# Scores of gated linear attention in three products of 128 columns per chunk

## The chip, the cores and the metric

The kernel runs on one core of a Trainium2 chip. The core has TensorE (PE, with its weight loads shown as PEld), VectorE (DVE), ScalarE (ACT), GpSimd (POOL) and SyncE (SP), which here issues all DMAs. The metric is the device time of one execution in microseconds; lower is better.

## What is computed

One layer of a hybrid backbone: a normalised input is projected once into eleven parts, from which a bidirectional gated linear attention (GLA, four heads of 128 key channels) and a differential attention are computed, gated, merged and projected out. The change concerns the scores inside a chunk of GLA, for one direction:

```python
cum = jnp.cumsum(log_a, axis=3)                       # chunks of 64 positions
ref = cum[:, :, :, GLA_CHUNK // 2 - 1:GLA_CHUNK // 2]
scores = jnp.einsum('bhnid,bhnjd->bhnij', q * jnp.exp(cum - ref), k * jnp.exp(ref - cum))
o_intra = jnp.einsum('bhnij,bhnjv->bhniv', jnp.where(tri, scores, 0.0), v)
o_inter = ...                                         # from the state carried between chunks
o = o_intra + o_inter                                 # forward; backward the same on reversed streams; the two are added
```

There are 1024 latent tokens and 256 context tokens, all in fp32.

## The kernel before

The kernel works with chunks of 128 positions, cut into two sub-chunks `s` of 64. A head has ten chunks, two of context and eight of latent tokens. The latent ones are worked on in pairs, `g` = 1 to 4, and `e` is the direction (0 forward, 1 backward). For a pair the scores of both directions are masked, added and stored to DRAM (`d_sc`) as one array of 128 x 128 per chunk.

A small planner writes the order of the instructions. Every task is a Python generator that says what it waits for; the planner keeps an estimated clock for each engine, and the order in which tasks are woken is the order of the instructions on TensorE, ACT, DVE and POOL. On the chip each engine then works its list off in that order, and semaphores hold it where an operand is late. Between the tasks of GLA, TensorE works on the stream of projections (tiles `mm`, `ma`, `tp`), which has the lowest priority and fills the gaps. Buffers are counted by tag: `acq` waits for a free one, `rel` gives it back. `TAGS` gives each tag its pool and number of buffers.

GLA's first part (`gla_a`, with the tiles of pool `sbG`) has these tasks for each head. `scans` forms the cumulated decays `cf` (forward) and `eb` (backward). `kstates` and `queries` form the operands of the carried state. `factors` subtracts a sub-chunk's reference from the decays (`gd` for a sub-chunk's own reference, `gx` for the other one's), `rest` takes Exp on ACT and multiplies with queries (`gqr`) and keys (`gkk`) on DVE or POOL, whichever the planner expects to be done first (`either`). `scores` then multiplies on TensorE into one PSUM bank `gs`, copies it to `gsc` on ACT, masks it on POOL (`affine_select`), adds the directions and stores. Before, a score product is 128 x 64: all of a chunk's keys, in the form that one sub-chunk of queries needs (its own block, the block beside the diagonal, zeros elsewhere), times that sub-chunk's queries. Eight such products serve a pair (two directions, two chunks, two sub-chunks). `gsc`, `gd` and `gx` have one buffer.

When the last scores are stored (`ev_ga`), `sums7` starts: it adds and subtracts blocks of the input activations for a stage of seven products per weight matrix, where TensorE uses `gs`, `go`, `gt` and `ma` for four tiles at a time. Its operand `s2` overwrites the second half of the activations (`h`); if the projections before it still need that half, `s2` goes to DRAM and is fetched back later. The first of the seven products is evacuated by ACT, the second is added to `us` and `rope` by DVE, the third is the one with `s2`.

Of the kernel before, what the change touches and what calls it, by code (L numbers as in the profile page):

```python
# [12 lines left out]
AF = mybir.ActivationFunctionType  # L13
ALU = mybir.AluOpType
# [5 lines left out]
P = 128  # L20
# [6 lines left out]
TAU = 1.0 / 16  # L27
# [218 lines left out]
class Hybrid:  # L246
# [10 lines left out]
        gk=("sbG", 2), gq=("sbG", 1), glab=("sbG", 2), glaf=("sbG", 2), gsc=("sbG", 1), gtl=("sbG", 4), gm=("sbG", 1),  # L257
        **{f"{t}{e}": ("sbG", n) for t, n in dict(ge=2, gkt=2, gqe=2, gqr=2, gkk=2, gd=1, gx=1).items() for e in range(2)},
# [1256 lines left out]
    def gla_a(self):  # L1515

        d = self.d
        H = [dict() for _ in range(4)]
        ev_s = {(h, e): Event() for h in range(4) for e in range(2)}
        ev_r = {(h, g, e): Event() for h in range(4) for g in range(1, 5) for e in range(2)}  # L1520
# [111 lines left out]
        def factors():  # L1632

            for h in range(4):
# [5 lines left out]
                for g in range(1, 5):  # L1640
                    for e in range(2):
                        sl = slice(2 * g, 2 * g + 2)
                        q4 = st["gq"][:, 2 * g - 2:2 * g].rearrange("p c (s t) -> p c s t", t=64)
                        k4 = st["gk"][:, sl].rearrange("p c (s t) -> p c s t", t=64)
                        cc = st["eb" if e else "cf"][:, sl].rearrange("p c (s t) -> p c s t", t=64)
                        ref = cc[:, :, :, 32:33] if e else cc[:, :, :, 31:32]
                        for tg in ("gd", "gx", "gqr", "gkk"):
                            yield from self.acq(f"{tg}{e}")
                        dd = self.t(f"gd{e}", [P, 2, 2, 64])
                        yield On(0, "DVE")  # L1650
                        for s in range(2):
                            self.dve.tensor_tensor(dd[:, :, s], cc[:, :, s], ref[:, :, s].to_broadcast([P, 2, 64]),
                                                   ALU.subtract)
                        xd = self.t(f"gx{e}", [P, 2, 64])
                        r_ = ref[:, :, 1 - e].to_broadcast([P, 2, 64])
                        x = (cc[:, :, 1], r_) if e else (r_, cc[:, :, 0])
                        self.dve.tensor_tensor(xd, *x, ALU.subtract)
                        qq = self.t(f"gqr{e}", [P, 2, 2, 64])
                        kk = self.t(f"gkk{e}", [P, 2, 4, 64])
                        self.pool.memset(kk[:, :, 2 if e else 1], 0.0)  # L1660
                        d.spawn(rest(h, g, e, dd, xd, qq, kk, q4, k4), d.on("ACT", dd), prio=2)

        def rest(h, g, e, dd, xd, qq, kk, q4, k4):
            sg = -1.0 if e else 1.0
            self.act.activation(qq, dd, AF.Exp, scale=sg * TAU)
            self.act.activation(dd, dd, AF.Exp, scale=-sg * TAU)
            self.act.activation(xd, xd, AF.Exp, scale=TAU)
            yield d.when(qq, H[h]["gq"])
            self.either(qq, q4, qq, ALU.mult)
            yield d.when(dd, H[h]["gk"])  # L1670
            self.rel(f"gd{e}", self.either(kk[:, :, 0:4:3], k4, dd, ALU.mult))
            yield d.when(xd)
            self.rel(f"gx{e}", self.either(kk[:, :, 1 if e else 2], k4[:, :, e], xd, ALU.mult))
            ev_r[h, g, e].qk = qq, kk
            d.set(ev_r[h, g, e], d.when(qq, kk))

        def scores():

            for h in range(4):
                for g in range(1, 5):  # L1680
                    for e in range(2):
                        yield ev_r[h, g, e]
# [997 lines left out]
```

## Time and profile before

| | us |
|---|---|
| median of three runs (1685.82 to 1686.82) | 1686.13 |
| the profiled execution | 1685.7 |
| its span | 1684.0 |
| TensorE busy | 1631.7 |
| VectorE busy | 1208.2 |
| ScalarE busy | 819.1 |
| GpSimd busy | 647.8 |

The profile is of one execution. Times in its timeline run from the start of the span; a row groups consecutive instructions of one kind, and its length reaches to the modelled end of the last one, so the pace is read from start to start. On TensorE an fp32 product of the scores is two records. What stands in brackets is idle time ahead of the row and the work whose end ended it.

### The profile page before, as it was taken

How to read it: one execution, taken by the hardware profiler on the slowest of the kernel's cores; microseconds unless marked ns; L12 is line 12 of the kernel's file. 1: busy time of each engine (PE TensorE's matmuls, PEld its weight loads, DVE VectorE, ACT ScalarE, POOL GpSimd, SP SyncE). 2: the span in 40 equal slices, each digit the busy share in tenths (PEclk: the TensorE clock that was granted, in tenths of full speed). 3: DMA queues.
4: the chain of work that ended last, by engine and by line, in shares of the span. 5: the costliest groups of instructions: out<-in, count | busy, mean ns of one | idle time of the engine just before them, and what ended most of it. 6: DMA issues, size and time to landing. Idle time of an engine off the chain costs nothing.

```text
span 1684.0 us, 24646 instructions
## 1 busy us (share of the span) xinstructions
PE 1631.7 (97%) x8381; PEld 1354.1 (80%) x8381; DVE 1208.2 (72%) x1940; ACT 819.1 (49%) x1633; POOL 647.8 (38%) x659
## 2 busy tenths in 40 slices
PE   8999999999999999999999989999999999999999
PEld 3688887888788878888888778888888888878887
DVE  4766867866855465857776658897888888847694
ACT  4786545454342434343332346665666565642231
POOL 1600542552310013435444625565655656630000
PEclk9999999999999999999999999999999999999999
DMA  8547554653754474459899663443784534257422
GB/s 312 204 154 238 172 165 164 190 160 125 232 170 138 143 237 140 143 174 279 270 301 314 184 196 107 111 128 85 222 262 114 157 105 125 66 180 251 152 99 75
DMA packets 266431, 296.58 MB, mean 176 GB/s; under 512 B 23577, under 2 KB 186305, under 8 KB 266305
## 3 DMA queue, kind: packets, MB, share of 16 engines
q1 hardware_dynamic: 266304, 295.01, 56.0%
q8 instruction: 66, 1.08, 0.3%
q14 instruction: 61, 0.49, 0.1%
HBM read 195.84 MB, written 99.09 MB: 175 GB/s over the span
## 4 chain that ended last, share of the span: by engine, by line
PE 71%; DVE 11%; POOL 5%; issue 4%; ACT 3%; DMA 2%; SPq 0%; ACTq 0%; POOLq 0%; DVEq 0%
PE mm L353 16%; PE mc L353 10%; PE ma L353 9%; PE s L353 6%; PE mb L353 6%; PE b L353 5%; PE gs L353 5%; DVE sm L211 4%; PE go L353 3%; PE b L379 3%; PE gt L353 3%; DVE e L211 2%; PE tp L353 2%; ACT e L211 2%; POOL p L211 2%
## 5 line engine op out<-in xcount | busy, mean ns | idle before, releaser
L211 DVE TENSOR_REDUCE sm<-s 128x1 f32<-128x1024 f32 (+1 forms) x192 | 197.3, 1037 | 33.1 <-PE s L353 32.5
L353 PE MATMUL mm<-w,h 128*128 128x512 f32 x864 | 216.9, 400 | 3.0 <-DVE w L211 2.3
L211 ACT ACTIVATE e<-s,sm 128x1280 f32<-128x1280 f32 x128 | 170.2, 1331 | 85.5 <-DVE sm L211 75.6
L353 PEld LDWEIGHTS mm<-w,h 128*128 128x128 f32 x864 | 160.7, 189 | 38.0 <-DVE w L211 2.6
L211 POOL TENSOR_TENSOR at<-ac,at 128x512 fp32r<-128x512 f32 x128 | 186.0, 1453 | 10.7
L353 PE MATMUL s<-kk,aq 128*128 128x512 f32 (+1 forms) x768 | 173.9, 360 | 6.9 <-ACT e L211 6.9
L353 PE MATMUL mb<-h,wt 128*128 128x512 f32 x624 | 170.5, 404 | 4.8 <-DVE ft L211 3.2
L211 POOL TENSOR_SCALAR at<-ac 128x512 fp32r<-128x512 f32 x128 | 97.5, 761 | 186.9 <-ACT ac L211 181.5
L353 PE MATMUL mm<-h,w 128*128 128x512 f32 x624 | 154.6, 398 | 0.0
L353 PEld LDWEIGHTS s<-kk,aq 128*128 128x128 f32 x768 | 121.0, 188 | 26.3 <-ACT e L211 10.7
L353 PEld LDWEIGHTS mm<-h,w 128*128 128x128 f32 x624 | 116.7, 191 | 24.1 <-DVE h L211 0.4
L353 PE MATMUL b<-at,vv 128*128 128x256 f32 x960 | 129.6, 283 | 1.9 <-DVE at L211 1.4
L353 PEld LDWEIGHTS mb<-h,wt 128*128 128x128 f32 x624 | 109.7, 188 | 25.2 <-DVE ft L211 4.3
L353 PEld LDWEIGHTS b<-at,vv 128*128 128x128 f32 x960 | 120.9, 188 | 7.4 <-POOL at L211 2.6
L211 POOL TENSOR_TENSOR sm<-sm,nhalf 128x8 f32<-128x8 f32 (+3 forms) x78 | 105.4, 1351 | 30.7 <-DVE sm L211 25.3
L353 PE MATMUL mc<-h,wt 128*128 128x512 f32 x480 | 113.1, 396 | 1.6 <-DVE wt L211 1.6
L211 DVE SCALAR_TENSOR_TENSOR e<-e,sm,e 128x1280 f32<-128x1280 f32 x64 | 112.4, 1756 | 1.2
L353 PEld LDWEIGHTS mc<-h,wt 128*128 128x128 f32 x480 | 90.9, 190 | 22.2 <-DVE wt L211 2.5
L211 ACT ACTIVATE ac<-b 128x512 f32<-128x512 f32 x121 | 71.9, 598 | 57.3 <-PE b L379 54.9
L353 PE MATMUL ma<-w,h 128*128 128x512 f32 x384 | 96.6, 396 | 0.4 <-DVE gp L211 0.4
L379 PE MATMUL b<-ident,e 128*128 128x128 f32 x604 | 87.6, 273 | 6.9 <-DVE at L211 3.1
L379 PEld LDWEIGHTS b<-ident,e 128*128 128x128 f32 x604 | 72.5, 141 | 23.8 <-ACT ac L211 3.9
(385 smaller groups left out, 3177.6 us busy)
## 6 DMA issues: line engine op xcount, KB each, us to landing
raw<-in_w_in SPq DMA_DIRECT2D x37, 512.0 KB, 4.7
rb<-in_w_in SPq DMA_DIRECT2D x64, 256.0 KB, 3.0
aq<-d_qT SPq DMA_DIRECT2D x128, 128.0 KB, 4.0
d_kT<-pl SPq DMA_DIRECT2D x40, 256.0 KB, 2.4
d_dv<-pl SPq DMA_DIRECT2D x40, 256.0 KB, 2.1
kk<-d_kT SPq DMA_DIRECT2D x32, 320.0 KB, 4.8
gv<-d_v SPq DMA_DIRECT2D x40, 256.0 KB, 4.5
vv<-d_dv SPq DMA_DIRECT2D x16, 640.0 KB, 6.6
```

What stands on the lines that cost most here:

```text
L211: self.ins = f(out, *args, **kw).ins
L353: self.ins = self.nc.tensor.matmul(out, lhsT, rhs, start=start, stop=stop, skip_group_check=more).ins
L379: self.nc.tensor.transpose(out, src, self.ident[:n, :n])
```

## The change

The factors of both directions now lie in joint tiles: `qq` [128, chunk, direction, sub-chunk, 64], `kk` the same, and `xx` [128, chunk, direction, 64] for the block beside the diagonal. Per chunk there are three products of 128 columns: for each direction all keys times all queries, each with its own sub-chunk's reference (only the two diagonal blocks of it are used), and one that holds the blocks beside the diagonal of both directions: 64 columns of keys of each direction, times the queries `q[:, 64:192]`, the forward second sub-chunk and the backward first one. A half pair (`j`) takes the bank `gs`, ACT copies the two full products and then, over them, the two 64 x 64 blocks of the third. So the bank is taken twice per pair, and emptied in six copies. The zeroing of parts of `gkk` falls away, and `gd` with it: the differences are formed in `kk`. `gsc`, `gqr`, `gkk` and `gx` have two buffers each.

```diff
@@ -254,8 +254,9 @@
 
         s7=("sbS", 24), ra=("sbS", 4), rb=("sbS", 3), us=("sbS", 2), rc=(None, 4), **{f"u{x}": (None, 1) for x in range(12)},
 
-        gk=("sbG", 2), gq=("sbG", 1), glab=("sbG", 2), glaf=("sbG", 2), gsc=("sbG", 1), gtl=("sbG", 4), gm=("sbG", 1),
-        **{f"{t}{e}": ("sbG", n) for t, n in dict(ge=2, gkt=2, gqe=2, gqr=2, gkk=2, gd=1, gx=1).items() for e in range(2)},
+        gk=("sbG", 2), gq=("sbG", 1), glab=("sbG", 2), glaf=("sbG", 2), gsc=("sbG", 2), gtl=("sbG", 4), gm=("sbG", 1),
+        gqr=("sbG", 2), gkk=("sbG", 2), gx=("sbG", 2),
+        **{f"{t}{e}": ("sbG", 2) for t in ("ge", "gkt", "gqe") for e in range(2)},
 
         bkt0=("sbA2", 2), bkt1=("sbA2", 2), gv0=("sbA2", 3), gv1=("sbA2", 3), bqe=("sbA2", 2), bsc=("sbA2", 3), bg=("sbA2", 3),
         gsb0=("sbA2", 8), gsb1=("sbA2", 8), gsf=("sbA2", 4), gs1=("sbA2", 1), gp=("sbA2", 4), gpl=("sbA2", 4),
@@ -1517,7 +1518,7 @@
         d = self.d
         H = [dict() for _ in range(4)]
         ev_s = {(h, e): Event() for h in range(4) for e in range(2)}
-        ev_r = {(h, g, e): Event() for h in range(4) for g in range(1, 5) for e in range(2)}
+        ev_r = {(h, g): Event() for h in range(4) for g in range(1, 5)}
         heads = [Event() for _ in range(4)]
         for h in range(4):
             for e in range(2):
@@ -1638,72 +1639,80 @@
                 while "gq" not in st:
                     yield At(d.now + 2.0)
                 for g in range(1, 5):
+                    for tg in ("gkk", "gx", "gqr"):
+                        yield from self.acq(tg)
+                    kk = self.t("gkk", [P, 2, 2, 2, 64])
+                    xx = self.t("gx", [P, 2, 2, 64])
+                    qq = self.t("gqr", [P, 2, 2, 2, 64])
                     for e in range(2):
-                        sl = slice(2 * g, 2 * g + 2)
-                        q4 = st["gq"][:, 2 * g - 2:2 * g].rearrange("p c (s t) -> p c s t", t=64)
-                        k4 = st["gk"][:, sl].rearrange("p c (s t) -> p c s t", t=64)
-                        cc = st["eb" if e else "cf"][:, sl].rearrange("p c (s t) -> p c s t", t=64)
+                        cc = st["eb" if e else "cf"][:, 2 * g:2 * g + 2].rearrange("p c (s t) -> p c s t", t=64)
                         ref = cc[:, :, :, 32:33] if e else cc[:, :, :, 31:32]
-                        for tg in ("gd", "gx", "gqr", "gkk"):
-                            yield from self.acq(f"{tg}{e}")
-                        dd = self.t(f"gd{e}", [P, 2, 2, 64])
+                        own = [cc, ref.to_broadcast([P, 2, 2, 64])]
+                        far = [ref[:, :, 1 - e].to_broadcast([P, 2, 64]), cc[:, :, e]]
                         yield On(0, "DVE")
-                        for s in range(2):
-                            self.dve.tensor_tensor(dd[:, :, s], cc[:, :, s], ref[:, :, s].to_broadcast([P, 2, 64]),
-                                                   ALU.subtract)
-                        xd = self.t(f"gx{e}", [P, 2, 64])
-                        r_ = ref[:, :, 1 - e].to_broadcast([P, 2, 64])
-                        x = (cc[:, :, 1], r_) if e else (r_, cc[:, :, 0])
-                        self.dve.tensor_tensor(xd, *x, ALU.subtract)
-                        qq = self.t(f"gqr{e}", [P, 2, 2, 64])
-                        kk = self.t(f"gkk{e}", [P, 2, 4, 64])
-                        self.pool.memset(kk[:, :, 2 if e else 1], 0.0)
-                        d.spawn(rest(h, g, e, dd, xd, qq, kk, q4, k4), d.on("ACT", dd), prio=2)
-
-        def rest(h, g, e, dd, xd, qq, kk, q4, k4):
-            sg = -1.0 if e else 1.0
-            self.act.activation(qq, dd, AF.Exp, scale=sg * TAU)
-            self.act.activation(dd, dd, AF.Exp, scale=-sg * TAU)
-            self.act.activation(xd, xd, AF.Exp, scale=TAU)
+                        self.dve.tensor_tensor(kk[:, :, e], *own[::-1 if e else 1], ALU.subtract)
+                        yield On(0, "DVE")
+                        self.dve.tensor_tensor(xx[:, :, e], *far[::-1 if e else 1], ALU.subtract)
+                    d.spawn(rest(h, g, kk, xx, qq), d.on("ACT", xx), prio=2)
+
+        def rest(h, g, kk, xx, qq):
+            k = H[h]["gk"][:, 2 * g:2 * g + 2]
+            both = lambda x: x.unsqueeze(2).to_broadcast([P, 2, 2, P])
+            flat = lambda x: x.rearrange("p c e s t -> p c e (s t)")
+            self.act.activation(qq, kk, AF.Exp, scale=TAU)
+            self.act.activation(kk, kk, AF.Exp, scale=-TAU)
+            self.act.activation(xx, xx, AF.Exp, scale=TAU)
             yield d.when(qq, H[h]["gq"])
-            self.either(qq, q4, qq, ALU.mult)
-            yield d.when(dd, H[h]["gk"])
-            self.rel(f"gd{e}", self.either(kk[:, :, 0:4:3], k4, dd, ALU.mult))
-            yield d.when(xd)
-            self.rel(f"gx{e}", self.either(kk[:, :, 1 if e else 2], k4[:, :, e], xd, ALU.mult))
-            ev_r[h, g, e].qk = qq, kk
-            d.set(ev_r[h, g, e], d.when(qq, kk))
+            self.either(flat(qq), both(H[h]["gq"][:, 2 * g - 2:2 * g]), flat(qq), ALU.mult)
+            yield d.when(kk, H[h]["gk"])
+            self.either(flat(kk), both(k), flat(kk), ALU.mult)
+            yield d.when(xx)
+            xf = xx.rearrange("p c e t -> p c (e t)")
+            self.either(xf, k, xf, ALU.mult)
+            ev_r[h, g].qk = qq, kk, xx
+            d.set(ev_r[h, g], d.when(qq, kk, xx))
 
         def scores():
+
+            def evac(j, psc, sc, after):
+                act = self.act.activation
+                act(sc[:, :, j], psc[:, 0:2], AF.Copy)
+                act(sc[0:64, 0, j, 64:128], psc[0:64, 2, 0:64], AF.Copy)
+                self.rel("gs", act(sc[64:128, 1, j, 0:64], psc[64:128, 2, 64:128], AF.Copy))
+                if j:
+                    d.spawn(after(sc), d.on("POOL", sc), prio=2)
+                return
+                yield
 
             for h in range(4):
                 for g in range(1, 5):
-                    for e in range(2):
-                        yield ev_r[h, g, e]
-                    yield from self.acq("gs")
-                    psc = self.t("gs", [P, 2, 2, 2, 64])
-                    for e in range(2):
-                        qq, kk = ev_r[h, g, e].qk
-                        for j in range(2):
-                            for s in range(2):
-                                en = self.mm(psc[:, e, j, s], kk[:, j, 2 * s:2 * s + 2].rearrange("p a b -> p (a b)"),
-                                             qq[:, j, s], True, True)
-                        self.rel(f"gqr{e}", en)
-                        self.rel(f"gkk{e}", en)
-                    yield On(en, "ACT")
+
+                    def sums(sc, h=h, g=g):
+                        for e in range(2):
+                            sg = -1 if e else 1
+                            self.pool.affine_select(sc[:, e], sc[:, e], pattern=[[0, 2], [sg, P]], compare_op=ALU.is_ge,
+                                                    fill=0.0, base=0, channel_multiplier=-sg)
+                        yield d.when(sc)
+                        self.either(sc[:, 0], sc[:, 0], sc[:, 1], ALU.add)
+                        self.store([(self.d_sc[h][:, 2 * g - 2:2 * g], sc[:, 0])], ("gsc", 1), ev=self.ev_st["sc", 0, h, g])
+                        finished(h)
+
+                    yield ev_r[h, g]
+                    qq, kk, xx = ev_r[h, g].qk
                     yield from self.acq("gsc")
                     sc = self.t("gsc", [P, 2, 2, P])
-                    en = self.act.activation(sc, psc.rearrange("p e j s t -> p e j (s t)"), AF.Copy)
-                    self.rel("gs", en)
-                    yield On(en, "POOL")
-                    for e in range(2):
-                        sg = -1 if e else 1
-                        self.pool.affine_select(sc[:, e], sc[:, e], pattern=[[0, 2], [sg, P]], compare_op=ALU.is_ge,
-                                                fill=0.0, base=0, channel_multiplier=-sg)
-                    yield d.when(sc)
-                    self.either(sc[:, 0], sc[:, 0], sc[:, 1], ALU.add)
-                    self.store([(self.d_sc[h][:, 2 * g - 2:2 * g], sc[:, 0])], ("gsc", 1), ev=self.ev_st["sc", 0, h, g])
-                    finished(h)
+                    for j in range(2):
+                        yield from self.acq("gs")
+                        psc = self.t("gs", [P, 3, P])
+                        q = qq[:, j].rearrange("p e s t -> p (e s t)")
+                        for e in range(2):
+                            self.mm(psc[:, e], kk[:, j, e].rearrange("p s t -> p (s t)"), q[:, e * P:(e + 1) * P], True, True)
+                        en = self.mm(psc[:, 2], xx[:, j].rearrange("p e t -> p (e t)"), q[:, 64:192], True, True)
+                        if j:
+                            for tg in ("gqr", "gkk", "gx"):
+                                self.rel(tg, en)
+                        d.spawn(evac(j, psc, sc, sums), On(en, "ACT"), prio=2)
+                        yield AtPE(0)
 
         mask = self.t("gm", [P, 5, P + 1])
         self.pool.memset(mask, 1.0)
```

Three places show what this does to the order. First TensorE, at the first scores of the first head; `go` and `tp` rows are transposes with `ident`, `mm` and `ma` rows products of the stream. Before:

```order
L379 MATMUL go_2318<-ident,ge_466_2283 128x128 x2
L353 MATMUL gs_2322<-gqr_413_2029,gkk_414_2030 128x64 x4
L353 MATMUL gs_2322<-gqr_454_2240,gkk_455_2241 128x64 x4
L379 MATMUL tp_2331<-ident,p_2251 128x128 x4
L353 MATMUL mm_2343<-w_1622,kk_230 128x512
L353 MATMUL mm_2343<-w_1623,kk_230 128x512
L353 MATMUL mm_2343<-w_1622,kk_230 128x512
```

The eight products stand in one block (two rows of four). The same place after the change, on TensorE:

```order
L354 MATMUL gs_2243<-gqr_1784,gkk_1782 128x128 x2
L354 MATMUL gs_2243<-gqr_1784,gx_1783 128x128
L380 MATMUL go_2247<-ident,ge_449_2191 128x128 x2
L354 MATMUL ma_2197<-w_1733,h_197_836 128x512
L354 MATMUL ma_2197<-w_1734,h_197_836 128x512
L354 MATMUL ma_2197<-w_1733,h_198_837 128x512
L354 MATMUL ma_2197<-w_1746,h_201_849 128x512
L354 MATMUL ma_2197<-w_1747,h_201_849 128x512
L354 MATMUL ma_2197<-w_1746,h_202_850 128x512
L354 MATMUL gs_2270<-gqr_1784,gkk_1782 128x128 x2
L354 MATMUL gs_2270<-gqr_1784,gx_1783 128x128
L354 MATMUL mm_2278<-w_1622,h_172_742 128x512
```

One block of eight products has become two of three, with six products of the stream between them.

Second ACT, at the copies of the first head's last pairs out of PSUM; `gqr`, `gd` (after: `gkk`) and `gx` rows are Exp of factors, `p` and `w` belong to the projections. Before, where `gsc_2686` is the third pair and `gsc_2739` the fourth:

```order
L211 ACTIVATE p_2662<-mm_2591 128x512
L211 ACTIVATE gsc_2686<-gs_2676 128x512
L211 ACTIVATE gqr_553_2692<-gd_550_2685 128x256
L211 ACTIVATE gd_550_2685<-gd_550_2685 128x256
L211 ACTIVATE gx_552_2690<-gx_552_2690 128x128
L211 ACTIVATE p_2730<-ma_2661 128x512
L211 ACTIVATE gsc_2739<-gs_2717 128x512
L211 ACTIVATE gqr_565_2767<-gd_563_2762 128x256
L211 ACTIVATE gd_563_2762<-gd_563_2762 128x256
L211 ACTIVATE gx_564_2765<-gx_564_2765 128x128
```

The fourth pair's copy is followed at once by the Exp of the next head's factors. The same place after, on ACT, where `gsc_2496` is the third pair and `gsc_2569` the fourth:

```order
L211 ACTIVATE gqr_2447<-gkk_2445 128x512
L211 ACTIVATE gkk_2445<-gkk_2445 128x512
L211 ACTIVATE gx_2446<-gx_2446 128x256
L211 ACTIVATE gsc_2496<-gs_2522 128x2x128
L211 ACTIVATE gsc_2496<-gs_2522 64x64 x2
L211 ACTIVATE w_2531<-raw_2456 128x512
L211 ACTIVATE p_2539<-mm_2360 128x512
L211 ACTIVATE p_2544<-ma_2361 128x512
L211 ACTIVATE w_2561<-raw_2456 128x512
L211 ACTIVATE gsc_2569<-gs_2570 128x2x128
L211 ACTIVATE gsc_2569<-gs_2570 64x64 x2
L211 ACTIVATE gsc_2569<-gs_2591 128x2x128
```

The Exp ahead are now the fourth pair's own, of both directions at once; the next head's have moved further back, and the copies come in threes, of 128 x 256 and twice 64 x 64 elements.

Third DVE, behind the scores, in the stage of seven products (`h_185` is the last of the four parts of `s2`, `us` and `rope` rows evacuate the second of the seven products, `pl`, `p`, `ra`, `raw`, `w` and `s` are other sums of that stage). Before:

```order
L211 TENSOR_TENSOR raw_4048<-rb_4714,ra_4698 128x512
L211 TENSOR_TENSOR rope_4546<-rope_4546,mm_4800 128x512
L211 TENSOR_TENSOR pl_4825<-h_184_789,h_185_790 128x512
L211 TENSOR_TENSOR w_4832<-raw_4048,w_4831 128x512
L211 TENSOR_TENSOR pl_4839<-h_150_640,h_151_641 128x512
L211 TENSOR_TENSOR pl_4827<-pl_4825,pl_4827 128x512
L211 TENSOR_TENSOR pl_4825<-pl_4779,pl_4825 128x512
L211 TENSOR_TENSOR w_4857<-ra_4607,w_4856 128x512
L211 TENSOR_TENSOR pl_4779<-pl_4827,pl_4779 128x512
L211 TENSOR_TENSOR w_4865<-ra_4615,w_4864 128x512
L211 TENSOR_TENSOR w_4872<-ra_4628,w_4871 128x512
L211 TENSOR_TENSOR h_185_790<-pl_4779,h_184_789 128x512
```

The last part of `s2` stands ten rows behind the last row with `rope` of the second product. After, on DVE, around the first row with `us`:

```order
L211 TENSOR_TENSOR h_185_790<-pl_4470,h_184_789 128x512
L211 TENSOR_TENSOR pl_4528<-pl_4528,pl_4470 128x512
L211 TENSOR_TENSOR w_4587<-raw_3979,w_4586 128x512
L211 TENSOR_TENSOR ra_4505<-ra_4505,raw_3980 128x512
L211 TENSOR_TENSOR s_867_4360<-p_4545,s_866_4359 128x512
L211 TENSOR_TENSOR w_4596<-raw_3979,w_4595 128x512
L211 TENSOR_TENSOR w_4604<-raw_3980,w_4603 128x512
L211 TENSOR_TENSOR h_173_743<-p_4570,h_172_742 128x512
L211 TENSOR_TENSOR s_900_4465<-p_4547,s_899_4464 128x512
L211 TENSOR_TENSOR us_4435<-us_4435,mm_4606 128x512
L211 TENSOR_TENSOR h_176_749<-p_4613,h_175_748 128x512
L211 TENSOR_TENSOR w_4651<-raw_3980,w_4650 128x512
```

`h_185` has moved ahead of the first row with `us`, and the two parts that come back from DRAM (`h_173`, `h_176`) stand beside it.

## Prediction

> **What bounds the kernel now.** I read the page first, then busy time by stretch, then the timeline of TensorE through the scores' stage, then the other engines where TensorE paused. From the page, the engine totals and the chain that ended last:
>
> ```profile
> PE 1631.7 (97%) x8381; PEld 1354.1 (80%) x8381; DVE 1208.2 (72%) x1940; ACT 819.1 (49%) x1633; POOL 647.8 (38%) x659
> PE 71%; DVE 11%; POOL 5%; issue 4%; ACT 3%; DMA 2%; SPq 0%; ACTq 0%; POOLq 0%; DVEq 0%
> ```
>
> TensorE is the bound over the span. The order of the changed kernel differs on TensorE only between the first factors (186 us) and the last products before the seven-product stage; further on every row names the same tiles. So the stretch to look at is 186 to 410 us, with what it hands on. Columns below: length, busy time of PE, PEld, DVE, ACT, POOL (instructions), granted clock, DMA share, GB/s.
>
> ```profile
> 186.00:410.00 224.00, 219.65 (x1142) 184.42 (x1141) 163.44 (x364) 115.03 (x306) 101.18 (x147) 0.98 0.48 152
> ```
>
> DVE, ACT and POOL have room on average (73, 51 and 45%). TensorE idles 4.35 us, and the clock is not quite 1. Both come from one place. Timeline of PE (start, length, output<-inputs, idle before and who ended it):
>
> ```profile
> 243.45 1.89 PE L353 MATMUL gs<-gqr,gkk 128*128 128x64 f32 x16
> 245.15 3.00 PE L353 MATMUL ma<-h,w 128*128 128x512 f32 x12
> 247.99 1.89 PE L353 MATMUL gs<-gqr,gkk 128*128 128x64 f32 x16
> 249.69 0.94 PE L353 MATMUL ma<-h,w 128*128 128x512 f32 x3
> 250.47 8.34 PE L353 MATMUL mm<-h,w 128*128 128x512 f32 x36
> 262.01 1.10 PE L353 MATMUL gs<-gqr,gkk 128*128 128x64 f32 x8 [3.20 <-POOL gkk L211]
> 263.48 1.97 PE L353 MATMUL gs<-gqr,gkk 128*128 128x64 f32 x8 [0.36 <-POOL gkk L211]
> 265.20 5.30 PE L353 MATMUL mm<-h,w 128*128 128x512 f32 x12
> 270.34 2.93 PE L353 MATMUL ma<-h,w 128*128 128x512 f32 x12
> ```
>
> A score block of a pair of chunks is 16 records and holds TensorE for 1.70 us (243.45 to 245.15). The fifth block waits 3.20 us, and then twelve products take 5.14 us instead of 2.84. The clock in the stretches after the wait:
>
> ```profile
> 265.20:270.30 5.10, 5.10 (x14) 4.03 (x14) 5.07 (x8) 1.70 (x6) 1.99 (x3) 0.51 0.07 23
> 270.30:275.00 4.70, 4.70 (x23) 3.79 (x22) 3.22 (x8) 4.11 (x14) 1.17 (x4) 1.00 0.40 140
> ```
>
> So a wait of 3.2 us costs as much again in halved clock. The Trainium skill (TensorE: Matmul & The Clock Gate, Part 1) says that an idle window of about 3.4 us halves the clock until one busy window has passed; the 0.51 here agrees. What made the wait, in the timelines of SP, ACT and POOL:
>
> ```profile
> 248.51 2.63 SPq L318 DMA_DIRECT2D gq<-d_q  x1
> 251.25 0.37 SPq L318 DMA_DIRECT2D d_sc<-gsc  x1
> 250.67 0.60 ACT L211 ACTIVATE p<-ma 128x512 f32<-128x512 f32 x1 [3.69 <-PE ma L353]
> 256.73 0.60 ACT L211 ACTIVATE gsc<-gs 128x512 f32<-128x512 f32 x1 [5.46 <-DMA d_sc<-gsc]
> 260.01 2.82 POOL L211 TENSOR_TENSOR gkk<-gk,gd 128x256 f32<-128x256 f32 x2 [1.56 <-ACT gd L211]
> ```
>
> The store of the third block's scores stood behind a head's loads. `gsc` has one buffer, so ACT waited 5.46 us for that store before it could take the fourth block out of PSUM; behind that stood the masks, their sum, the next factors, and with them the fifth block.
>
> A second loss lies just behind the stage, in the product with `s2`, whose operands (`h`, second half) are made only when the scores are done:
>
> ```profile
> 417.65 2.88 PE L353 MATMUL go<-w,h 128*128 128x512 f32 x12
> 420.37 2.88 PE L353 MATMUL gt<-w,h 128*128 128x512 f32 x12
> 447.57 2.20 PE L353 MATMUL gs<-w,h 128*128 128x512 f32 x9
> 451.84 0.73 PE L353 MATMUL gs<-w,h 128*128 128x512 f32 x2 [2.07 <-ACT h L211]
> 452.99 0.50 PE L353 MATMUL gs<-w,h 128*128 128x512 f32 x1 [0.41 <-DVE h L211]
> 453.33 2.89 PE L353 MATMUL go<-w,h 128*128 128x512 f32 x12
> ```
>
> Twelve such products need 2.72 us (417.65 to 420.37, 0.227 each); these took 5.76.
>
> **The change, part by part.** (a) *Products.* Per pair of chunks, eight products of 64 columns become six of 128. A product is two records here (16 records for eight). The trace has no plain product of 128 columns with these types; the neighbour on the other side has 256:
>
> ```profile
> 816.25 0.59 PE L353 MATMUL go<-gsf,bqe 128*128 128x256 f32 x2
> 816.68 0.59 PE L353 MATMUL go<-gv,bsc 128*128 128x256 f32 x2
> ```
>
> That is 0.43 us for two records, 0.215 each, against 1.70/16 = 0.106 with 64 columns. If columns set the price, 128 cost 0.1075, hardly more than 64, which then sit on a floor; if the price rises in a straight line from 64 to 256, they cost 0.142. I take 0.1075. The Trainium skill (TensorE: Matmul & The Clock Gate, "LDWEIGHTS") gives 128/1.2 = 107 ns for loading a full set of weights whatever follows, which agrees with a floor at 0.106. Before: 16 x 1.70 = 27.2 us. After: 16 x 12 x 0.1075 = 20.6. Gain 6.6, with ends of 0 (0.142) and 6.8 (0.106). All of it is on TensorE, which is the path.
>
> (b) *More turns.* The scores now come as 32 blocks of three products, and the order puts stream products between the halves of each pair: foreign blocks between stream products rise from 50 to 67. The first stream products after a block cost extra: 2.84 against 2.72 (245.15 to 247.99), or 0.78 against 0.68 (249.69 to 250.47). So +17 x 0.11 = +1.9 us (1.7 to 2.0).
>
> (c) *Two buffers for* `gsc`. The copy out of PSUM waits for the store of two blocks before. In the changed ACT order the fourth block's copies come with the second block's store as their condition, and the fifth block stands 54 stream products (12 us) behind the fourth. I take the wait at 262 us as gone. Its worth: 36 x 0.227 from 250.47, one block of 1.70 and twelve products at 2.84 end at 263.2; they ended at 270.34. Gain 7.2, with 0 as the other end, if another wait of this kind takes its place.
>
> (d) *The scores end earlier.* With two buffers for everything in the factors, the last score block stands 45 stream products (10.2 us) further from the end of the projections. The sums and `s2` move forward with it: all four `s2` parts now stand ahead of the second `us<-us,mm` on DVE, where the last one stood behind the second `rope<-rope,mm`. Two of them take a detour through DRAM (two stores, two loads more on SP), with those 10 us as cover. Gain 5.76 - 2.72 = 3.0; other end 0.
>
> (e) *ACT.* Prices by form between 180 and 412 us (busy, mean ns):
>
> ```profile
> L211 ACT ACTIVATE w<-raw 128x512 fp32r<-128x512 f32 x28 | 17.1, 625 | 2.2 <-PE mm L353 2.2
> L211 ACT ACTIVATE gd<-gd 128x256 f32<-128x256 f32 x32 | 13.4, 419 | 1.3
> L211 ACT ACTIVATE gqr<-gd 128x256 f32<-128x256 f32 x32 | 13.1, 411 | 8.6 <-DVE gd L211 8.6
> L211 ACT ACTIVATE gsc<-gs 128x512 f32<-128x512 f32 x16 | 9.5, 591 | 19.9 <-PE gs L353 7.8 <-DMA d_sc<-gsc 5.7 <-issue 4.4
> L211 ACT ACTIVATE gx<-gx 128x128 f32<-128x128 f32 x32 | 9.4, 293 | 0.0
> L211 ACT ACTIVATE gkt<-go 128x256 f32<-128x256 f32 x17 | 6.4, 377 | 4.0 <-PE go L379 4.0
> L211 ACT ACTIVATE dec<-glaf 128x10 f32<-128x10 f32 x3 | 0.6, 216 | 0.9 <-DVE glaf L211 0.9
> ```
>
> Per pair, six Exp and one copy (2 x 1.12 + 0.59 = 2.84 us) become three Exp (0.63 + 0.63 + 0.41) and six copies (2 x (0.38 + 2 x 0.22)), 3.31. That is 0.47 more, 7.5 us in all on an engine with 109 idle: off the path.
>
> (f) *DVE and POOL.* The same elements pass in fewer, longer instructions (four subtractions for six or more, three multiplications for six), and two memsets a pair go:
>
> ```profile
> L211 POOL MEMSET gkk<- 128x128 f32 x32 | 5.8, 203 | 0.0
> ```
>
> Nothing on the path; should their room go, the factors come late and TensorE waits as at 262 us.
>
> (g) *New waits.* `gs` stays one bank, and now each pair's second half waits until ACT has emptied it. The other waits of the stage come to 4.35 - 3.56 = 0.8 us for 50 foreign blocks; for 67, and with that bank, I add 1.0 (0 to 7.2, the price of one wait like that at 262).
>
> Sum: -6.6 + 1.9 - 7.2 - 3.0 + 1.0 = -13.9 us. The profiled execution took 1685.7 (span 1684.0); the median of the runs is 1686.13. I predict 1672 against that median. A change under 0.2% (3.4 us) can hardly be told from none here.
>
> **The rivals.** *Gain given back:* the products and turns as above, but another wait with half clock elsewhere. For it: static queues, and every DMA moved. Against: only one in 224 us before. -13.9 + 7.2 - 1.0: 1679 to 1680.
>
> *128 columns on the straight line:* (a) gives 0, so 1679. For it: no row excludes it. Against: the 64-column records are as short as half of a 256-column one.
>
> *Columns all the way down:* the Trainium skill (TensorE: Matmul & The Clock Gate, "Back-to-back issue gap") prices a product by N/2.4 plus a constant. By that, six products of 128 cost more than eight of 64. Worked from rows: 64-column records at 0.054 would make the old scores 13.8 us, (a) a loss of 6.8, and the time 1685.6, within 0.2% of before. The 1.70 us for 16 records speaks against it.
>
> *Slower: ACT late at the one bank.* After a block's end ACT takes 0.28 to start (block ends 245.15, copy starts 245.43) and 0.82 for three copies:
>
> ```profile
> 245.43 0.60 ACT L211 ACTIVATE gsc<-gs 128x512 f32<-128x512 f32 x1 [2.30 <-PE gs L353]
> ```
>
> The order leaves at least six stream products, 1.47 us with the turn, so 0.37 to spare. If instead the three Exp (1.67 us) stand ahead of the copies each time, TensorE waits 1.3 us per pair, 21 us in all: 1693. It decides from 0.87 us per pair (13.9/16). For it: ACT works strictly in order. Against: the changed ACT order mostly keeps the Exp behind the copies.
>
> *Doesn't do what it says:* the stage holds the same 713 stream products either way, so nothing but (c) and (d) could be missing: both waits stay, and only -4.7 + 1.0 is left: 1682.5.
>
> **How the numbers follow.** Forecast 0.58 (1668 to 1676: (a) and (b) at their ends, (g) between 0 and 4); gain given back 0.14; straight line 0.10; both waits stay 0.06; columns all the way 0.02; slower 0.06; the rest, a larger gain than seen here, 0.04. The range 1667 to 1683 leaves out the last two and the column case. Faster by over 0.2%: 0.88 (the first three, the larger gain, and a third of the both-stay case, which lies on the border); within: 0.06; slower: 0.06.
>
> **What would show it.** Score blocks of six records with 0.65 us from start to start (0.85 would be the straight line); no wait over 1 us on `gs` before 410 us and a granted clock of 1.00 throughout the stage; no wait for `h` in the first product with `s2`; scores ending some 10 us ahead of their old place in the stream. I am wrong if ACT's three copies make TensorE wait at the second halves, or a store behind a head's loads stops ACT again.

## The result, and the profile after

The changed kernel takes 1671.9 us (median of four runs, 1670.1 to 1672.1) against 1686.5 in the same comparison; the ratio is 0.9906, interval 0.9888 to 0.9924. The forecast was 1672. The profiled execution took 1671.8, its span 1670.1, so span against span it is 13.9 us, the sum that was predicted. The terms behind it did not all come out so. Ahead of the changed stage, where the order is the same, this execution was 0.7 us behind that of the kernel before.

The engine totals after:

```profile
PE 1621.8 (97%) x8317; PEld 1344.4 (81%) x8317; DVE 1203.2 (72%) x1868; ACT 832.1 (50%) x1665; POOL 642.7 (38%) x619
```

TensorE is still the bound, with 9.9 us less work shown. The score stage in busy time by stretch:

```profile
186.00:410.00 224.00, 221.88 (x1130) 184.71 (x1129) 178.52 (x315) 131.26 (x345) 108.97 (x115) 1.00 0.57 178
```

It idles 2.12 us instead of 4.35, and the clock is full. The waits of TensorE in that stretch (the view of waits: total, times, longest), of before the largest, of after all four:

```profile
PE gs L353 <- POOL gkk L211: 3.6, 2, 3.2
```
```profile
PE tp L380 <- POOL p L211: 0.7, 2, 0.5
PE gs L354 <- POOL gx L211: 0.7, 1, 0.7
PE gs L354 <- ACT gsc L211: 0.4, 1, 0.4
PE gt L380 <- POOL ge L211: 0.3, 1, 0.3
```

The wait of 3.2 us with the halved clock behind it has gone; five small ones, 2.1 us in all, stand in its place. A pair of chunks on TensorE, timeline after:

```profile
315.91 0.61 PE L354 MATMUL gs<-gqr,gkk 128*128 128x128 f32 x4
316.35 0.39 PE L354 MATMUL gs<-gqr,gx 128*128 128x128 f32 x2
316.50 1.64 PE L354 MATMUL mm<-w,h 128*128 128x512 f32 x6
317.97 0.60 PE L354 MATMUL gs<-gqr,gkk 128*128 128x128 f32 x4
```

Six records take 0.59 us (315.91 to 316.50), the six stream products behind them 1.47, which is 0.11 over their pace. Within the block the pace is 0.11 per record (four records from 315.91 to 316.35); the last product shows less, 0.15 to the start of the stream. The end of the scores and the seven-product stage, before (two rows) and after:

```profile
402.57 1.64 PE L353 MATMUL ma<-h,w 128*128 128x512 f32 x6
...
414.93 1.29 PE L353 MATMUL gs<-w,h 128*128 128x512 f32 x5
```
```profile
381.20 6.42 PE L354 MATMUL mm<-h,w 128*128 128x512 f32 x27
...
403.78 2.88 PE L354 MATMUL gs<-w,h 128*128 128x512 f32 x12
...
427.02 5.76 PE L354 MATMUL mm<-w,h 128*128 128x512 f32 x24 [1.32 <-DVE us L211]
...
438.05 2.88 PE L354 MATMUL gs<-w,h 128*128 128x512 f32 x12
440.77 2.88 PE L354 MATMUL go<-w,h 128*128 128x512 f32 x12
```

The scores now end 22.6 us ahead of the seven-product stage instead of 12.4, and the product with `s2` (438.05) takes 2.72 us without a wait. A wait of 1.32 us for `us` (to which DVE adds the second of the seven products) is new.

### The profile page after: what moved, and what is told of

It reads as the page before. It is cut to its first block, busy times and chain, and to the rows that moved or that the text cites. A ratio compares the mean times of both kernels' runs of the same rounds, so it can differ in the third digit from the quotient of the medians.

```text
span 1670.1 us, 24453 instructions
## 1 busy us (share of the span) xinstructions
PE 1621.8 (97%) x8317; PEld 1344.4 (81%) x8317; DVE 1203.2 (72%) x1868; ACT 832.1 (50%) x1665; POOL 642.7 (38%) x619
## 4 chain that ended last, share of the span: by engine, by line
PE 55%; DVE 10%; POOL 3%; issue 3%; ACT 3%; DMA 1%; SPq 0%; ACTq 0%; DVEq 0%; POOLq 0%
PE mc L354 10%; PE mm L354 7%; PE s L354 6%; PE mb L354 6%; PE b L354 5%; PE ma L354 5%; DVE sm L211 4%; PE go L354 3%; PE b L380 3%; PE gs L354 3%; PE gt L354 3%; PE tp L354 2%; DVE e L211 2%; ACT e L211 2%; POOL p L211 1%
```

## The experiments

The last two columns are read from TensorE's timeline: from the transposes at about 171 us, which have the same place in every kernel, to the first of the seven products, and from there to the end of the product with `s2`. Each ratio is against runs of the kernel before in the same comparison, whose median was 1686.5 to 1687.8. The edits are shown shortened to the words that differ.

| kernel | median us | ratio to before, interval | to the sevens | to the end of `s2` |
|---|---|---|---|---|
| before | 1686.5 | | 244.6 | 38.4 |
| changed | 1671.9 | 0.9906 (0.9888 to 0.9924) | 232.7 | 37.0 |
| e9 changed, again | 1670.6 | 0.9904 (0.9890 to 0.9917) | 232.7 | 36.9 |
| e1 one `gsc` | 1702.7 | 1.0093 (1.0081 to 1.0105) | 252.1 | 45.7 |
| e2 old products, two `gsc` | 1677.4 | 0.9945 (0.9932 to 0.9959) | 243.4 | 35.4 |
| e3 split into 64 columns | 1692.6 | 1.0028 (1.0019 to 1.0037) | 252.3 | 37.0 |
| e4 products twice | 1694.6 | 1.0039 (1.0024 to 1.0053) | 252.5 | 36.9 |
| e5 more turns | 1684.3 | 0.9982 (0.9973 to 0.9991) | 235.5 | 45.7 |
| e6 one factor buffer | 1684.8 | 0.9985 (0.9975 to 0.9995) | 235.9 | 46.3 |
| e7 one block per pair | 1673.8 | 0.9918 (0.9904 to 0.9932) | 236.3 | 35.4 |
| e8 copies twice | 1690.0 | 1.0014 (1.0005 to 1.0023) | 251.3 | 37.0 |
| e10 `gx` on DVE | 1673.2 | 0.9919 (0.9905 to 0.9934) | 234.0 | 37.0 |
| e11 one block, factors on DVE | 1674.2 | 0.9926 (0.9912 to 0.9941) | 237.6 | 35.4 |

Only e2, e3 and e9 came out within the range of their theory. The other eight were slower than theirs, e4 by 0.6 us and e10 by 0.2, the rest by more.

**The price of a product: e3 and e4.** In e3 each product of 128 columns becomes two of 64; in e4 each is issued twice. The order around them is that of the changed kernel.

```diff
-    self.mm(psc[:, x], kq, q[:, o:o + 128], True, True)
+    for y in range(2):                                    # e3
+        self.nc.tensor.matmul(psc[:, x, y * 64:(y + 1) * 64], kq, q[:, o + 64 * y:o + 64 * y + 64], start=True, stop=True)
+    self.nc.tensor.matmul(psc[:, x], kq, q[:, o:o + 128], start=True, stop=True)    # e4, ahead of the same product
```

> The changed kernel with each product of 128 columns issued as two of 64 columns, in the same order around them: twelve records more per half pair, 192 in place of 96 products. Theory (a record of 64 columns costs TensorE what one of 128 does, about 0.107 us): 192 more records, + 20.5, so 1692, range 1688 to 1694; a half pair's block of 12 records takes 1.2 to 1.3 us. Rival (columns set the price): the block stays at 0.59 to 0.7 us and the time at 1672 to 1678.

> The changed kernel with each product of 128 columns issued twice into the same place, in the same order around them. Theory (128 columns cost 0.107 us per record, all of it on the path): 192 records, + 20.6, so 1692, range 1688 to 1694, the same as with the split within 2 us. Rival (straight line from 64 to 256 columns, 0.142 per record): + 27, 1699. Rival (waits of the stage hide behind the added work): 1684 to 1688.

A half pair's block of twelve records in the timeline of e3, and of e4:

```profile
327.10 1.00 PE L1713 MATMUL gs<-gqr,gkk 128*128 128x64 f32 x8
327.94 0.61 PE L1713 MATMUL gs<-gqr,gx 128*128 128x64 f32 x4
328.36 1.63 PE L354 MATMUL mm<-w,h 128*128 128x512 f32 x6
```
```profile
327.64 0.38 PE L1712 MATMUL gs<-gqr,gkk 128*128 128x128 f32 x2
...
328.89 1.62 PE L354 MATMUL mm<-w,h 128*128 128x512 f32 x6
```

1.26 us for twelve records of 64 columns, 1.25 for twelve of 128: 0.105 and 0.104 each. Half the columns save nothing, and all of the added work is on the path: the stage grows by 19.6 and 19.8 us. The rest of + 20.7 and + 22.7 lies further on, where both kernels also met the long form of a wait that e9 takes up. The straight line and the columns' price are out. The Trainium skill (TensorE: Matmul & The Clock Gate, "LDWEIGHTS") puts the load of 128 weight columns at 128/1.2 = 107 ns, by the weight columns alone; the 0.105 and 0.104 of the two blocks are near it.

**The score buffer: e1 and e2.** e1 takes the second `gsc` out of the changed kernel, e2 gives it to the kernel before.

```diff
-gsc=("sbG", 2)    # e1, changed kernel
+gsc=("sbG", 1)
-gsc=("sbG", 1)    # e2, kernel before; gqe=2 becomes gqe=1 to make room
+gsc=("sbG", 2)
```

> The changed kernel with one buffer for gsc instead of two; products, factors and copies as changed. Theory (the second buffer carries term (c), and by ending the scores earlier term (d)): the copies out of the bank wait for the store of the pair before, the scores end at the edge of the seven-product stage, and the product with s2 waits again. 1671.9 + 7.2 + 3.0 = 1682, range 1677 to 1688, with a wait of over 2 us on gs or its factors in the score stage and a granted clock under 1 there. Rival (the products carry the gain, and the planner moves the rest out of the way): 1671 to 1675.

> The kernel before with two buffers for gsc and nothing else of the change: eight products of 64 columns in one block per pair, old factors. To make room, the two operands gqe of the carried state get one buffer each instead of two. Theory (terms (c) and (d) are the buffer's, (a) and (b) the products'): the wait of 3.2 us and its half clock go, the scores end 78 stream products earlier, s2 is ready: 1686.5 - 7.2 - 3.0 = 1676, range 1674 to 1680. Rival (the buffer alone does nothing, since other waits of the old factors take its place): 1684 to 1688.

e1 is slower than before, by far more than expected. Its last pairs on TensorE, and on ACT:

```profile
401.56 0.71 PE L354 MATMUL gs<-gqr,gkk 128*128 128x128 f32 x4 [0.30 <-ACT gsc L211]
...
407.71 1.22 PE L354 MATMUL gs<-gqr,gkk 128*128 128x128 f32 x4 [5.21 <-ACT gsc L211]
...
414.79 1.22 PE L354 MATMUL gs<-gqr,gkk 128*128 128x128 f32 x4 [2.82 <-ACT gsc L211]
...
423.79 5.49 PE L354 MATMUL gs<-w,h 128*128 128x512 f32 x12 [0.96 <-ACT gsc L211]
...
467.57 2.10 PE L354 MATMUL gs<-w,h 128*128 128x512 f32 x3 [4.12 <-ACT h L211]
```
```profile
406.79 0.86 ACT L211 ACTIVATE gsc<-gs 128x256 f32<-128x256 f32 x3 [1.48 <-DMA d_sc<-gsc]
...
420.26 0.86 ACT L211 ACTIVATE gsc<-gs 128x256 f32<-128x256 f32 x3 [2.91 <-DMA d_sc<-gsc]
```

With one buffer a pair needs its copies, masks, sum and store done before the next pair's first copy, 6.4 to 7.1 us per pair (407.71, 414.79, 421.18). The stream's filler ends first, and the last 22 us are scores alone, with TensorE waiting and its clock at a half (twelve products in 5.3 us at 423.79); then `s2` is late as well. In the old layout one bank held a whole pair, so one `gsc` cost a wait only where the store was late; two half pairs through one bank need the buffer between the halves. So the second buffer is needed, and its price of 10 us was too small by 21. But the loss is not where the theory had it: from 186 to 401 us the clock is 1.00 and the longest wait on `gsc` 1.5 us, so that the wait of the kernel before at 262 us does not come back with the single buffer.

e2 landed where the theory put it (1677.4 for 1676), but not by its terms. `s2` is in time (35.4 against 38.4: - 3.0, as expected). The stage itself gained only 1.1 us, since other waits came where that of 262 us had been:

```profile
291.69 1.10 PE L353 MATMUL gs<-gqr,gkk 128*128 128x64 f32 x8 [0.72 <-POOL gkk L211]
296.10 0.44 PE L379 MATMUL gt<-ident,ge 128*128 128x128 f32 x2 [1.85 <-DVE ge L211]
```

In the stretch behind them the clock was 0.56. The other 4.8 us lie behind the `s2` product: 2.6 of them between 465 and 620 us of the kernel before, where e9 finds a wait of two lengths, and 1.6 near 1516 us, where only the kernel before ran at a reduced clock (0.57 from 1516 to 1520). What the single `gqe` adds to those waits was not separated.

**Where the scores end: e5 and e6.** e5 lets the stream in between the products of a half pair; e6 takes the second factor buffers away.

```diff
     self.mm(psc[:, e], kk[:, j, e]..., True, True)
+    yield AtPE(d.now + 0.05)                              # e5
-gqr=("sbG", 2), gkk=("sbG", 2), gx=("sbG", 2)
+gqr=("sbG", 1), gkk=("sbG", 1), gx=("sbG", 1)             # e6
```

> The changed kernel with TensorE handed back to the stream behind each single score product, so that the same 96 products stand in up to 96 blocks instead of 32; foreign blocks between stream products rise by 46 over the changed kernel, and the last scores stand 72 stream products later (40 ahead of the seven-product stage). Theory of term (b) (a turn from foreign records back to the stream costs 0.11 us): + 46 x 0.11 = 5.1, so 1677; where s2 is late again by it, up to 3 more: range 1675 to 1681. Rival (turns cost nothing, the 0.11 is work of the score block itself): 1671 to 1673 with s2 in time.

> The changed kernel with one buffer each for gqr, gkk and gx, and still two for gsc. The same number of blocks and turns; the last scores stand 78 stream products later, 34 ahead of the seven-product stage. Theory (where the scores end decides whether s2 is ready, term (d), while the second factor buffers are worth nothing inside the stage): the product with s2 waits again, + 3.0, so 1675, range 1673 to 1678. Rival (s2 is in time with 34 products or 7.7 us to spare): 1671 to 1673. Rival (one factor buffer starves TensorE in the stage, as at 262 us before): 1679 or more.

Both lose most of the gain, and at the same place. The product with `s2` in e6:

```profile
402.04 2.31 PE L354 MATMUL mm<-h,w 128*128 128x512 f32 x9
...
451.36 2.03 PE L354 MATMUL gs<-w,h 128*128 128x512 f32 x3 [6.90 <-ACT h L211]
```

The last operand comes 49.3 us after the last score block (402.04 to 451.36); in the kernel before it was 50.4 (402.57 to 452.99), in e5 50.1. In the changed kernel DVE writes the last part of `s2` at

```profile
426.89 0.68 DVE L211 TENSOR_TENSOR h<-p,h 128x512 fp32r<-128x512 f32 x1
```

which ends 46.4 us after the last score block, and TensorE asks for it 56.9 us after (381.20 to 438.05); e6 asks after 38.4 (402.04 to 440.44). So the sums took 46 to 50 us in these four kernels, while the products ahead of the need differ, and the sooner TensorE is through its stage, the sooner it stands waiting for them: `s2` costs 9.3 us in e6, three times as much as before the change. The wait was foreseen; its price of 3.0 was that of the old, slower stage, and the last scores stand only 21 stream products ahead of the sevens in e6 and 27 in e5, where 34 and 40 had been counted. e6 loses another 3.2 us in the stage.

e5 also prices the turn. One product at a time, timeline of TensorE:

```profile
380.49 0.38 PE L354 MATMUL gs<-gqr,gkk 128*128 128x128 f32 x2
380.62 0.94 PE L354 MATMUL mm<-h,w 128*128 128x512 f32 x3
381.40 0.38 PE L354 MATMUL gs<-gqr,gkk 128*128 128x128 f32 x2
```

Two records show 0.13 to 0.14 and the three products behind them 0.78 instead of 0.68: 0.24 together, 0.12 per record. In a block of six it is 0.59 + 0.11 = 0.70, also 0.12. The 0.11 behind a block is thus mostly the unshown rest of its last product (0.14 shown where 0.22 is the pace), and by this estimate a turn costs 0.02 to 0.03 us. The 46 turns then cost about 1 us of the 2.8 that the stage lost; the rest is waits, on `p` from POOL above all (2.8 us against 0.7). The rival was nearer on the turn. Of the 12 us that the kernel lost, 8.7 are the late `s2`.

**ACT at the one bank: e8.**

```diff
     act = self.act.activation
+    raw = self.nc.scalar.activation      # the same three copies once more, ahead
+    raw(sc[:, :, j], psc[:, 0:2], AF.Copy)
+    raw(sc[0:64, 0, j, 64:128], psc[0:64, 2, 0:64], AF.Copy)
+    raw(sc[64:128, 1, j, 0:64], psc[64:128, 2, 64:128], AF.Copy)
```

> The changed kernel with ACT's three copies of each half pair out of gs issued twice, in the same order around them: 1.64 us instead of 0.82. It prices the rival of ACT late at the one bank. Theory (0.37 us to spare with six stream products between the halves): 0.28 + 1.64 - 1.47 = 0.45 us of wait in about 15 of the 32 blocks, + 6.8, so 1678.6, range 1676 to 1681, clock 1.00. Rival (the waits draw the clock down): 1684 or more. Rival (the bank has more to spare than worked out): 1671 to 1673.

```profile
230.97 0.94 PE L354 MATMUL ma<-w,kk 128*128 128x512 f32 x3
...
233.06 0.71 PE L354 MATMUL gs<-gqr,gkk 128*128 128x128 f32 x4 [0.46 <-ACT gsc L211]
...
240.93 0.71 PE L354 MATMUL gs<-gqr,gkk 128*128 128x128 f32 x4 [1.60 <-ACT gsc L211]
```

Where nothing else stands on ACT the wait is 0.46, against 0.45 worked out, and TensorE goes from block to block in 2.09 us instead of 1.47, 0.62 more. But ACT does its list in order: at the wait at 240.93 it had an operand and two tiles of the stream to do first, and its copies started at 239.12, 1.4 us after the block's end at 237.69. The waits on `gsc` come to 9.2 us in 18 places, those on `gx` and `ge` grew to 1.7 and 1.5, and in all it costs 18.1 us, or 1.13 per pair, at full clock in the stage. The slower rival's point of decision, 0.87 per pair, is consistent with that: this kernel ends a little behind the one before. The expectation counted one kind of wait and fell short: each wait costs TensorE some 0.16 us more than its length (0.62 against 0.46), and ACT's delay reached other operands. About 3 of the 18.1 us were not traced to a row.

**The rest, and two tries to go further: e9, e7, e10, e11.** e9 is the changed kernel once more. e7 puts the second half into the bank `gt`, so that a pair is one block; e10 has the `gx` multiplication on DVE; e11 is e7 with all three factor multiplications on DVE.

```diff
+    for tg in ("gt", "gs"):                               # e7, e11: both banks, then all six products
+        yield from self.acq(tg)
-    psc = self.t("gs", [P, 3, P])
+    psc = self.t(("gs", "gt")[j], [P, 3, P])
-    self.either(xf, k, xf, ALU.mult)
+    self.dve.tensor_tensor(xf, k, xf, ALU.mult)           # e10; e11 also for gqr and gkk
```

> The changed kernel itself, unaltered, as the yardstick for the two beside it and to see whether the wait ahead of the 38 stream products behind the sevens (1.26 us at full clock in its first profile, 2.08 to 2.48 us with a lower clock in two kernels with the same order) changes between executions of one order. Theory (it does, by 2 to 3 us, and is no part of the change): 1672, range 1669 to 1675. Rival (it is the same in every execution): 1671 to 1673.

> The changed kernel with the second half of each pair in the bank gt, so that both halves' six products stand in one block and the bank gs is no longer waited for between the halves: 16 blocks instead of 32, 10 turns fewer in all, the last scores 15 stream products later. Theory: 10 x 0.11 = 1.1 and the waits on gs of 0.4 us less: 1670.4, range 1669 to 1672. Rival (gt is wanted by the transposes, which wait): 1673 to 1678.

> The changed kernel with the multiplication of gx with the keys always on DVE instead of DVE or POOL; the last scores stand where they stood. Theory (the remaining waits of the stage, 0.69 us for gx from POOL and 0.36 behind it, come from POOL products of 128 x 256 that take 1.6 us on average and up to 3.4): 1.0 to 1.5 us less, 1670.6, range 1668 to 1673. Rival (DVE hands the delay on to other waits): 1672 to 1675.

> One block per pair (second half in the bank gt) and all three factor multiplications always on DVE. The last scores stand 6 stream products later than in the changed kernel, 106 ahead of the seven-product stage. Theory (the waits of 1.67 us for gkk and 2.53 us for p in the one-block kernel came from factor products on POOL): those two go, the wait for us of 1.3 us stays away: 1673.8 - 4.2 = 1669.6, range 1667 to 1672. Rival (DVE becomes late instead, and s2 with it): 1674 to 1680.

e9 bears on a wait far behind the change, at the stream's 38 products after the sevens. The row of before, then those of changed, e9, e3 and e8, which have one and the same order there:

```profile
610.03 10.55 PE L353 MATMUL mm<-w,h 128*128 128x512 f32 x38 [2.33 <-DVE w L211]
```
```profile
595.79 9.29 PE L354 MATMUL mm<-w,h 128*128 128x512 f32 x38 [1.26 <-DVE w L211]
```
```profile
596.19 9.27 PE L354 MATMUL mm<-w,h 128*128 128x512 f32 x38 [1.15 <-DVE w L211]
```
```profile
617.17 10.50 PE L354 MATMUL mm<-w,h 128*128 128x512 f32 x38 [2.48 <-DVE w L211]
```
```profile
614.43 9.23 PE L354 MATMUL mm<-w,h 128*128 128x512 f32 x38 [1.08 <-DVE w L211]
```

So there is a short form (1.1 to 1.3 us, full clock) and a long one (2.1 to 2.5, then a reduced clock), some 2.4 us apart, and one order shows both in different kernels. The same kernel twice gave the short form, so that it changes between executions of one kernel is not shown; that the order alone does not decide it, is.

None of the other three beats the changed kernel; their intervals overlap with its own. In e7 and e11 the last scores stand 129 and 138 stream products ahead of the sevens, against 99 in the changed kernel, so they came earlier and not, as expected, 15 and 6 products later. e7 lost its wait for `us` (35.4 against 37.0) and paid in the stage, with waits for `gkk` and `p` from POOL:

```profile
286.19 0.71 PE L354 MATMUL gs<-gqr,gkk 128*128 128x128 f32 x4 [1.67 <-POOL gkk L211]
...
369.10 0.66 PE L380 MATMUL tp<-ident,p 128*128 128x128 f32 x4 [2.53 <-POOL p L211]
```

e11 removed the first and kept 1.66 us of the second, with new waits of 0.77 and 0.83 for weights and a clock of 0.82 from 292 to 296 us; e10 lost the wait for `gx` and got 0.61 for `gqr`. Each time a multiplication moved from POOL to DVE made something else late.

## Why the prediction was right

*(a) and (b), products and turns.* Predicted - 6.6 + 1.9 = - 4.7. A block with the 0.11 behind it went from 16 x 1.81 to 32 x 0.70: - 6.6 us together. The price of a record was right (taken as 0.1075; 0.104 by block in e3 and e4, 0.11 by the pace within one). The step that failed is (b): the 0.11 was charged as a price of the turn, while most of it belongs to the block's last product. At 0.11 a record the 64 records saved are worth 7.0, and 17 turns at 0.03 cost 0.5, an estimate from these rows. The total was therefore under-sized by 2.

*(c) and (g), the store wait and the new ones.* Predicted - 7.2 + 1.0. The wait is gone and the clock is 1.00, as forecast; the other waits of the stage are 2.1 us, where 0.8 stood before: + 1.3. By the whole stage (- 11.9, of which products and turns take 6.6) the two come to - 5.3 where - 6.2 was forecast. What took the wait away is not settled. e1 has one buffer and the wait at 262 us is not there; e2 has two, among the old products, and gains only 1.1 in the stage. The effect of (c) is shown, its cause in the second buffer alone is not: the new order of factors and copies may be enough for this wait, and where e1 shows the buffer to be needed is the end of the stage.

*(d), `s2`.* The product went from 5.76 to 2.72 as predicted. Not foreseen was the next late thing, the 1.32 us for `us`, whose evacuation now stands behind the operands of `s2` on DVE; 1.4 us net remained. And e6 shows how much hangs on (d): with the scores ending 21 stream products ahead of the sevens the faster stage loses 9 us there, which is most of what it won.

*(e), (f), ACT, DVE and POOL.* Off the path, but for 0.36 us behind ACT's copies and one product on POOL. The wait of 0.69 us for `gx` came from this row:

```profile
281.81 3.42 POOL L211 TENSOR_TENSOR gx<-gk,gx 128x256 f32<-128x256 f32 x1 [4.57 <-ACT gx L211]
```
```profile
281.48 0.69 DVE L211 TENSOR_TENSOR gqr<-gq,gqr 128x512 f32<-128x512 f32 x1
282.08 0.69 DVE L211 TENSOR_TENSOR gkk<-gk,gkk 128x512 f32<-128x512 f32 x1
...
283.96 1.82 DVE L211 TENSOR_TENSOR w<-raw,w 128x512 fp32r<-128x512 f32 x2
```
```profile
L211 POOL TENSOR_TENSOR ge<-gk,ge 128x256 f32<-128x256 f32 x7 | 5.4, 774 | 12.8 <-ACT ge L211 12.8
```

The same shape takes 0.77 on average for `ge` (last row, by groups); this one, the slowest of seven, stood beside a run of two-input instructions on DVE, one behind the other from 281.5 on, and ended at 285.23, within the last row shown, whose two instructions took 1.82 us where one takes 0.69. The Trainium skill (SBUF — State Buffer, "SBUF: two separate sides") has DVE with two inputs and GpSimd take turns at one pair of ports, each for a whole instruction; the row agrees with that, and no run here tests it alone.

*The rivals.* Straight line and columns fell with e3 and e4. ACT at the one bank cost 0.36 us once; e8 shows that it was near. Gain given back did not occur within the stage, and both waits of the kernel before went.

*Behind the change* 1.3 us more went, which no term had: - 3.0 up to 788 us, most of it the long form at the 38 products giving way to the short one, and + 1.7 further on. The sum of the working, - 13.9, was met by - 11.9 in the stage, - 1.4 at `s2` and - 1.3 behind, with 0.7 lost ahead of the stage. That total is partly luck: the 1.9 more from products and turns and the 2.5 less from (c), (g) and (d) nearly cancel, and so, in part, do the 1.3 behind the change and the 0.7 ahead of it, which stood in no term. The lower end of the forecast range, 1668, also does not follow from the terms: (a) at 6.8, (b) at 1.7 and (g) at 0 give 1670.8.

## What to carry to other kernels

Count small fp32 products by records, not by columns: here 64 and 128 columns cost the same, so filling a product to 128 saves time and splitting it buys nothing. Before a stage is made faster, measure how long what it feeds takes on the other engines; if the consumer's operands need 46 to 50 us after the stage's last work, the speed is worth something only if that work moves forward too. And in this kernel two halves through one bank needed double buffers on both sides of it: each single buffer taken back (e1, e6) lost nearly all of the gain or more, much of it further on, at `s2`.

## What the runs showed of the hardware

The clock does not follow from the length of a wait alone. In e2 the wait of 1.85 us was followed by a clock of 0.56 over 3 us; in e7 the wait of 2.53 us was followed by 1.00:

```profile
297.00:300.00 3.00, 3.00 (x10) 2.23 (x9) 3.00 (x6) 1.42 (x5) 0.00 (x0) 0.56 0.53 141
```
```profile
369.00:372.00 3.00, 2.90 (x17) 2.51 (x18) 0.89 (x2) 2.14 (x6) 1.77 (x4) 1.00 0.21 59
```

The changed kernel and e9, one kernel run twice, show it without any change of order. At 1309 us both have waited for the same operand, for 1.82 us in the first and 1.70 in the second, and only the second runs on at a reduced clock. The row and the busy time by stretch, of changed and of e9:

```profile
1308.81 1.65 PE L354 MATMUL mb<-h,wt 128*128 128x512 f32 x6 [1.82 <-DVE ft L211]
1309.00:1313.00 4.00, 4.00 (x22) 3.38 (x22) 3.10 (x5) 1.16 (x4) 3.41 (x3) 1.00 0.42 139
```
```profile
1308.92 2.62 PE L354 MATMUL mb<-h,wt 128*128 128x512 f32 x6 [1.70 <-DVE ft L211]
1309.00:1313.00 4.00, 4.00 (x11) 3.08 (x12) 2.77 (x4) 0.25 (x1) 3.30 (x3) 0.57 0.40 133
```

From 1502 to 1506 us it is the other way round, 0.57 in the first and 1.00 in the second, each behind a wait of 1.46. So part of what separates two executions is where the reduced clock falls.

The Trainium skill (TensorE: Matmul & The Clock Gate, Part 1) describes a window of 3.4 us that runs freely. That the same wait may or may not cost the clock agrees with a free-running window; that 1.85 us in e2 and 1.70 in e9 were enough does not agree with one whole idle window. A rule "a wait of so many us halves the clock" cannot be read from one case.
